# A written order for VectorE, ScalarE and SyncE from the output projection on, and the first down tile multiplied out of the first pool of weights

## The chip, the core and the metric

One core of a Trainium2 chip. The metric is the device time of one execution in microseconds (us). The engines of the core are TensorE (PE, matmuls and transposes), VectorE (DVE), ScalarE (ACT), GpSimd (POOL) and SyncE (SP), which here only issues DMA transfers.

## The reference, cut to what matters

One decoder layer on 256 tokens of width 2048, everything in float32:

```python
h = rmsnorm(x, mix_pre_gain)
q_a, k_a, v_a, q_r, f_r, i_r, g_r = split(h @ w_in)          # 2048 x 5376
attn = rmsnorm(sliding_window_attention(q_a, k_a, v_a, sinks), attn_out_gain)
rnn = hgrn2_chunkwise(q_r, f_r, i_r, g_r, lb, rnn_norm_gain)
mixed = concat([attn, rnn], -1) @ w_out                      # 2048 x 2048
x = x + rmsnorm(mixed, mix_post_gain)
h = rmsnorm(x, mlp_pre_gain)
u = relu(h @ w_up)                                           # 2048 x 8192
y = (u * u) @ w_down                                         # 8192 x 2048
x = x + rmsnorm(y, mlp_post_gain)
```

The change touches the stretch from the last quarter of `@ w_out` to the first products of `@ w_down`.

## The kernel before, in words

**Products in three parts.** Every float32 operand is split into a high part (`whi`, a cast to a shorter format, on ACT, line 90) and a low part (`wlo`, the rest, a subtraction on DVE, line 91). A product is three matmuls: high x high, high x low, low x high (`three`, lines 111 to 113, or `product`, line 785). Weights come in tiles of 512 rows by 512 columns, 1 MB, held as 128 partitions x 4 x 512. Such a raw tile is loaded by a DMA on SP's queue, cast on ACT, subtracted on DVE, and only then can PE use it.

**Tokens.** The 256 tokens are two blocks of 128 (`tb` 0 and 1). `wide_step(o, ch, aT, tb, kt)` multiplies the activations of one block, rows `128*kt` on, by 512 columns of weights into one bank of PSUM: three matmuls. A product of one block over all 2048 rows has 16 such steps, 48 matmuls.

**Output projection (lines 648 to 687).** The 2048 columns are four blocks of 512. The first three are done for both token blocks in turn. From line 660 on PE's order is the written one (`manual_schedule` for PE). The last column block does token block 0, then block 1. `evac_post(c, tb, bank)` squares the bank on ACT for the norm and multiplies it by the gain on DVE into `acc` (tile `mg`, line 608). After the last column `residual(tb)` (line 614) makes the factor (a sum on DVE, a power on POOL, line 600) and adds the scaled rows to `x2` in four DVE steps of 512 columns (line 618), then stores `x2` to memory. `norm2(tb)` (line 635) squares `x2` in four ACT steps (line 589), sums (lines 640, 641), takes a power on POOL (line 642), and makes the normalised rows `hn` in four DVE steps (line 645). `turn(tb, c)` transposes 512 columns of `hn` on PE (four transposes, line 627) into a bank tagged `sc`, casts it to the high part on ACT (line 629) and subtracts for the low part on DVE (line 630), into `h2T`.

**First up chunk (lines 689 to 768).** The 8192 hidden columns are eight chunks of 1024. Of chunk 0, the first 512 columns are multiplied for block 0, then block 1 (`up_w`, loaded at line 689 in half tiles); the next 512 columns (line 745) for both blocks in turn. In between PE turns `hn` of block 0 among the steps 9, 11, 13 and 15 of the last output block, and `hn` of block 1 among the steps 12 to 15 of the first up block. Results pass `relu` (ACT, line 667) and `turn_u` (line 669: four transposes, a square and a cast on ACT, a subtraction on DVE) into `uT`. DVE also makes sums and differences of `hn` (lines 746, 747, 756, 757), since the chunks 1 to 7 use a scheme of seven products for a 2 x 2 block product; `turn_sum` turns these as `s1`, `s2`, `s3`, `s4`.

**Pools of weights.** Up to line 771 weights live in the pool `wpool_a`: 3 raw tiles, 4 `whi`, 4 `wlo`. Then this pool and `phase_b` (with `x2`) are closed, and `wpool_c` opens on the same memory: 2 raw tiles each of the tags `d`, `X`, `P`, `Q`, 3 `whi`, 3 `wlo`. A new tile waits until the old tiles on its memory are done with.

**PSUM.** Eight banks: 3 tagged `pj`, 3 tagged `sc`, 1 `tr`, 1 `o`. A down product of both token blocks holds two banks `sc` from its first tile to its second (`down_half`, line 826).

**Segments (lines 843 to 1036).** From chunk 1 on the work is a list of segments, each one weight tile: up products (`X`, `P`, `Q`, `R`) of 12 matmuls and down tiles (`d`) of 24. From line 1013 on DVE, ACT and SP also follow the written order. For segment k the loop emits: the evictions of k-1 and the additions of raw tiles on DVE, the split of segment k+2 (`prepare`, cast on ACT, subtraction on DVE), evictions on ACT and the turns, the matmuls of k, then loads. Between lines 687 and 1013 the order of DVE, ACT and SP is chosen by a planner with a timing model of its own.

For chunk 1 the list `q` begins with the first down tile `dn[0][0]`, to which the two turns of `s4` are attached, then `m1_first[0]`, `m1_first[1]`, `dn[0][1]`.

Of the kernel before, what the change touches and what calls it, by code (L numbers as in the profile page):

```python
# [29 lines left out]
def tile_hybrid_layer(  # L30
# [36 lines left out]
    def nm(s):  # L67
        uid[0] += 1
        return f"{s}{uid[0]}"
# [110 lines left out]
    def small(shape, tag, bufs=2):  # L180
        return cpool.tile([P] + list(shape), F32, tag=tag, name=nm(tag), bufs=bufs)
# [405 lines left out]
    def square(src, dst):  # L587
        junk = upool.tile([P, 512], F32, tag="u2", name=nm("junk"), bufs=2)
        nc.scalar.activation(out=junk, in_=src, func=AF.Square, scale=D ** -0.5, accum_out=dst)
# [7 lines left out]
    def rsq_part(last, p):  # L597
        r = small([1], "rf")
        nc.vector.tensor_tensor(out=r, in0=last, in1=p, op=ALU.add)
        nc.gpsimd.tensor_tensor(out=r, in0=r, in1=mhalf[:, 0:1], op=ALU.pow)  # L600
        return r
# [11 lines left out]

    def residual(tb):
        r = rsq_part(pss[tb][:, 3:4], ppart[:, tb:tb + 1])
        for c in range(4):
            cs = slice(c * 512, (c + 1) * 512)
            nc.vector.scalar_tensor_tensor(out=x2[tb][:, cs], in0=acc[tb][:, cs], scalar=r, in1=x2[tb][:, cs],
                                           op0=ALU.mult, op1=ALU.add)
        nc.sync.dma_start(out=x2_dram[tb], in_=x2[tb])  # L620
        hn[tb] = keep.tile([P, D], F32, tag=f"acc{tb}", name=nm("hn"))


# [7 lines left out]

    def turn(tb, c):
        turn_act(hn[tb][:, c * 512:(c + 1) * 512], *(h2T[c][:, :, i, tb * P:(tb + 1) * P] for i in range(2)))

    def norm2(tb):
        s2 = small([4], f"s2{tb}")
        for c in range(4):
            square(x2[tb][:, c * 512:(c + 1) * 512], s2[:, c:c + 1])
        st = small([1], "st")
        nc.vector.reduce_sum(out=st, in_=s2, axis=AX.X)  # L640
        nc.vector.tensor_scalar(out=st, in0=st, scalar1=EPS, scalar2=None, op0=ALU.add)
        nc.gpsimd.tensor_tensor(out=rh[:, tb:tb + 1], in0=st, in1=mhalf[:, 0:1], op=ALU.pow)
        for c in range(4):
            cs = slice(c * 512, (c + 1) * 512)
            nc.vector.scalar_tensor_tensor(out=hn[tb][:, cs], in0=x2[tb][:, cs], scalar=rh[:, tb:tb + 1], in1=gpre[c],
                                           op0=ALU.mult, op1=ALU.mult)

    for c in range(3):
        ch = load_wide(w_out_v, 0, c * 512)
# [29 lines left out]
    def new_uT(first="mu0", second="mu1"):  # L679
        return [hpool.tile([P, 4, 2, S], F32R, tag=t, name=nm("uT")) for t in (first, second)]  # L680

    ch = load_wide(w_out_v, 0, 3 * 512, pieces=2)
    banks = [bank("pj"), bank("pj")]
    for kt in range(NKT):
        wide_step(banks[0], ch, mixT, 0, kt)
    evac_post(3, 0, banks[0])
    residual(0)
    norm2(0)
    up_w = load_wide(w_up_v, 0, 0, pieces=2)
    for kt in range(NKT):  # L690
        if kt in (9, 11, 13, 15):
            turn(0, (kt - 9) // 2)
        wide_step(banks[1], ch, mixT, 1, kt)
    evac_post(3, 1, banks[1])
    residual(1)
    norm2(1)


    uT = new_uT()
    ps = [bank("pj"), bank("pj")]  # L700
    for kt in range(NKT):
        if kt in (12, 13, 14, 15):
            turn(1, kt - 12)
        wide_step(ps[0], up_w, h2T, 0, kt)
    u = [new_u(), new_u()]
    relu(u[0], ps[0])
    for kt in range(NKT):
        if kt == 4:
            turn_u(uT, 0, 0, u[0], "tr", 1)
        wide_step(ps[1], up_w, h2T, 1, kt)  # L710
    relu(u[1], ps[1])

# [27 lines left out]
    in_h2T("a22", 1, 1)  # L742
    in_h2T("s4", 1, 0)

    up_w = load_wide(w_up_v, 0, 512)
    nc.vector.tensor_sub(out=tmp, in0=half(1, 0), in1=half(1, 1))
    nc.vector.tensor_sub(out=half(1, 0), in0=half(0, 0), in1=half(1, 0))
    ps = [bank("pj"), bank("pj")]
    for i in range(4):
        for tb in range(2):  # L750
            if i == 0 and tb == 1:
                turn_u(uT, 0, 1, u[1], "tr", 1)
            if i == 1:
                turn_sum(("s1", tmp), tb)
                if tb == 1:
                    nc.vector.tensor_sub(out=tmp, in0=tmp, in1=half(0, 0))
                    nc.vector.tensor_add(out=half(0, 0), in0=half(0, 1), in1=tmp)
            if i == 2:
                turn_sum(("s3", half(1, 0)), tb)
            if i == 3:  # L760
                turn_sum(("s2", tmp), tb)
            for j in range(4):
                wide_step(ps[tb], up_w, h2T, tb, 4 * i + j)
    prev = {}
    for tb in range(2):
        u = new_u()
        relu(u, ps[tb])
        prev[1, tb] = u

    pb.__exit__(None, None, None)  # L770
    pool_w.__exit__(None, None, None)
    wp[0] = ctx.enter_context(tc.tile_pool(name="wpool_c", bufs=2, side="right", reuse_waits="tile"))

    def raw_tile(tag, wv, kt0, c0):
        t = wp[0].tile([P, 4, 512], F32, tag=tag, name=nm(tag), bufs=2)
# [50 lines left out]
    def down_half(ch, c, h, uT, w, tbs=(0, 1), evac=True):  # L826
        if c == 3 and not held:
            held.extend([bank("o", 1), bank("tr", 1)])
        if h == 0 and 0 in tbs:
            down_banks[c] = held if c == 3 else [bank("sc"), bank("sc")]  # L830
        banks = down_banks[c]
        for tb in tbs:
            for j in range(4):
                kt = 4 * h + j
                first = kt == 0 and (c < 3 or ch == 0)
                last = kt == 7 and (c < 3 or ch == NCH - 1)
                three(banks[tb], tok(uT, kt, tb), (w[0][:, j, :], w[1][:, j, :]), first, last)
            if h == 1 and evac:
                evac_down(ch, c, tb, banks[tb])

# [57 lines left out]
    def period(ch, m1_next):  # L900
# [6 lines left out]
        m2 = [up_seg("R", ch, h, "c", lambda: sums["a12"], True) for h in range(2)]  # L907
        dn = [[down_seg(d, c, h) for h in range(2)] for c in range(4)]
        if ch == 1:
            q = [dn[0][0], m1_first[0], m1_first[1], dn[0][1], m5[0], m5[1], dn[1][0], m6[0], m6[1], dn[1][1],  # L910
                 m7[0], m7[1], dn[2][0], m3[0], m3[1], dn[2][1], m4[0], m4[1], m2[0], m2[1],
                 m1_next[0], dn[3][0], m1_next[1], dn[3][1]]
        else:
            q = [m5[0], m5[1], dn[0][0], m6[0], m6[1], dn[0][1], m7[0], m7[1], dn[1][0], m3[0], m3[1], dn[1][1],
                 m4[0], m4[1], dn[2][0], m2[0], m2[1], dn[2][1], m1_next[0], dn[3][0], m1_next[1], dn[3][1]]
# [25 lines left out]
        for k, to, frm, c, h in plan:  # L941
            q[k].adds.append(plus(to, frm, c, h))
        if ch == 1:
            q[0].turns += [lambda c=c: turn_sum(("s4", half(0, 0)), c) for c in range(2)]
            q[1].turns.append(t(d, 1, 0, d))
            q[2].turns.append(t(d, 1, 1, d))
            loads = [(0, "d", d, 1, 0), (1, "d", d, 1, 1), (4, "d", d, 2, 0), (7, "d", d, 2, 1),
                     (8, "R", ch, 0), (9, "R", ch, 1), (10, "d", d, 3, 0), (11, "Q", nx, 0), (12, "Q", nx, 1),
                     (13, "d", d, 3, 1), (14, "X", nx, 0), (15, "X", nx, 1), (16, "P", nx, 0), (17, "P", nx, 1),
                     (19, "d", ch, 0, 0), (21, "d", ch, 0, 1)]  # L950
        else:
            q[0].turns += [t(d, 0, 0, d), t(d, 0, 1, d)]
            q[3].turns.append(t(d, 1, 0, d))
            q[4].turns.append(t(d, 1, 1, d))
            loads = [(0, "d", d, 1, 0), (3, "d", d, 1, 1), (5, "R", ch, 0), (6, "R", ch, 1), (6, "d", d, 2, 0),
                     (9, "d", d, 2, 1), (12, "d", d, 3, 0), (15, "d", d, 3, 1),
                     (17, "d", ch, 0, 0), (19, "d", ch, 0, 1)]
            if nx < NCH:
                loads += [(8, "Q", nx, 0), (9, "Q", nx, 1), (11, "X", nx, 0), (12, "X", nx, 1), (14, "P", nx, 0),
                          (15, "P", nx, 1)]  # L960
# [49 lines left out]
    n_end = len(segs) + len(end)  # L1010
    segs += end + [Seg(lambda h=h: raws["d", last, 3, h], None) for h in range(2)]

    order_all = tc.manual_schedule(engines={mybir.EngineType.DVE, mybir.EngineType.Activation, mybir.EngineType.SP})
    order_all.__enter__()
    load_down(0, 0, 0)
    for h in range(2):
        load_up("X", 1, h)
    load_down(0, 0, 1)
    for h in range(2):
        load_up("P", 1, h)  # L1020

    def prepare(k, between=None):
        segs[k].w = split_weight(None, segs[k].raw(), bufs=3, between=between)

    prepare(0, lambda: [load_up("Q", 1, h) for h in range(2)])
    prepare(1)
    for k in range(n_end):
        x = segs[k]
        for f in (segs[k - 1].dve if k else []) + x.adds:
            f()  # L1030
        prepare(k + 2)
        for f in (segs[k - 1].act if k else []) + x.turns:
            f()
        x.pe(x.w)
        for f in x.loads:
            f()
# [36 lines left out]
```

## Time and profile before

| what | value |
|---|---|
| time, median of 3 runs | 1118.68 us (1118.08 to 1118.79) |
| the profiled execution | 1118.42 us |
| its span, first to last instruction | 1116.7 us |
| mean granted clock of TensorE | 0.990 |
| output projection, last column block, block 0 done | about 396.5 us from the start of the span |
| second token block of the first up block done | about 443 us |
| chunk 0 of the up product done | about 468 us |

How to read the profile: the page's busy times say how long each engine worked, and the chain which work ended last. The table of waits has, for an engine and an operation, what ended its idle time: total, times and longest, in us. A timeline has one line for an instruction, or for several alike in a row: start, duration (of all, first start to last end), engine, line, operation, output <- inputs, shape, count; behind it in brackets the idle time before it and what ended it. Matmuls overlap: the next starts before the last has ended.

### The profile page before, as it was taken

The page shows a single profiled execution, that of the slowest core. Times are in us where ns is not written, and L with a number is a line of the kernel's source. Part 1 is how long each engine was busy: PE and PEld are TensorE (multiplying, and loading weights), DVE is VectorE, ACT ScalarE, POOL GpSimd, SP SyncE. Part 2 cuts the span into 40 slices and gives each one's busy share as a digit, 9 for nine tenths or more (in the row PEclk, how much of TensorE's full clock was granted, in tenths as well). Part 3 has the DMA queues.
Part 4 walks back from the last instruction along what each step waited for, and adds up shares of the span by engine and source line. Part 5 has one row for each costly group of instructions (what it writes and reads, how often), then busy time and mean ns, then how long its engine had stood idle before and what let it go on. Part 6 is the DMA issues. An engine that isn't in the chain of part 4 may idle for free.

```text
span 1116.7 us, 14041 instructions
## 1 busy us (share of the span) xinstructions
PE 1086.6 (97%) x5708; PEld 926.3 (83%) x5708; DVE 846.1 (76%) x765; ACT 623.1 (56%) x719; POOL 19.8 (2%) x48
## 2 busy tenths in 40 slices
PE   8999989999999989899999999999999999999996
PEld 7999889999988867778788888888888888888885
DVE  6755666665655557498998898898898898898565
ACT  6554565545454445455675575575575575575542
POOL 2100000000000000000000000000000000000000
PEclk9999989999999989999999999999999999999999
DMA  8743424444458645726728638638638638534662
GB/s 270 246 164 115 151 76 152 151 151 151 152 190 311 215 158 183 263 83 222 259 92 284 227 99 281 223 103 279 220 108 277 218 112 277 214 114 151 236 253 76
DMA packets 125538, 209.61 MB, mean 188 GB/s; under 512 B 3945, under 2 KB 49570, under 8 KB 124450
## 3 DMA queue, kind: packets, MB, share of 16 engines
q1 hardware_dynamic: 125474, 208.72, 54.7%
q8 instruction: 45, 0.74, 0.3%
q14 instruction: 19, 0.16, 0.0%
HBM read 204.51 MB, written 4.19 MB: 187 GB/s over the span
## 4 chain that ended last, share of the span: by engine, by line
PE 89%; DVE 4%; ACT 2%; issue 1%; DMA 1%; POOL 0%; DVEq 0%; POOLq 0%; ACTq 0%
PE pj L785 21%; PE pj L112 10%; PE pj L113 10%; PE pj L111 10%; PE sc L112 8%; PE sc L111 8%; PE sc L113 8%; DVE wlo L91 2%; PE o L112 1%; PE o L113 1%; PE tr L112 1%; PE tr L113 1%; PE tr L111 1%; PE o L111 1%; ACT whi L90 1%
## 5 line engine op out<-in xcount | busy, mean ns | idle before, releaser
L91 DVE TENSOR_TENSOR wlo<-raw,whi 128x2048 fp32r<-128x2048 f32 (+2 forms) x84 | 152.8, 1832 | 74.6 <-ACT whi L90 74.3
L90 ACT CAST whi<-d 128x2048 fp32r<-128x2048 f32 x60 | 114.8, 1913 | 120.5 <-PE sc L113 85.9
L91 DVE TENSOR_TENSOR wlo<-d,whi 128x2048 fp32r<-128x2048 f32 x60 | 137.4, 2290 | 55.3 <-ACT whi L90 55.2
L90 ACT CAST whi<-raw 128x2048 fp32r<-128x2048 f32 (+2 forms) x84 | 127.8, 1539 | 77.4 <-PE pj L113 38.3
L112 PE MATMUL sc<-wlo,uT 128*128 128x512 f32 x384 | 150.5, 392 | 2.5 <-DVE wlo L91 2.5
L111 PE MATMUL sc<-whi,uT 128*128 128x512 f32 x384 | 150.5, 392 | 2.2 <-ACT whi L90 1.6
L113 PE MATMUL sc<-whi,uT 128*128 128x512 f32 x384 | 150.3, 391 | 0.4 <-DVE uT L677 0.4
L90 ACT CAST whi<-X 128x2048 fp32r<-128x2048 f32 x56 | 107.1, 1915 | 77.9 <-DVE X L789 32.3
L785 PE MATMUL pj<-whi,hT 128*128 128x512 f32 x448 | 143.9, 390 | 0.0
L91 DVE TENSOR_TENSOR wlo<-X,whi 128x2048 fp32r<-128x2048 f32 x56 | 127.9, 2286 | 2.5 <-ACT whi L90 2.5
L111 PE MATMUL pj<-hT,whi 128*128 128x256 f32 x384 | 110.5, 288 | 1.1 <-ACT whi L90 0.7
L113 PE MATMUL pj<-hT,wlo 128*128 128x256 f32 x384 | 110.5, 288 | 0.9 <-DVE wlo L91 0.8
L112 PE MATMUL pj<-hT,whi 128*128 128x256 f32 x384 | 111.2, 290 | 0.0
L785 PE MATMUL pj<-whi,a 128*128 128x512 f32 x336 | 109.9, 395 | 0.0
L785 PEld LDWEIGHTS pj<-whi,hT 128*128 128x128 f32 x448 | 84.1, 188 | 17.4
L112 PEld LDWEIGHTS sc<-wlo,uT 128*128 128x128 f32 x384 | 72.5, 189 | 18.3 <-DVE wlo L91 3.4
L111 PEld LDWEIGHTS sc<-whi,uT 128*128 128x128 f32 x384 | 72.4, 189 | 18.0 <-ACT whi L90 1.8
L785 PE MATMUL pj<-wlo,hT 128*128 128x512 f32 x224 | 87.2, 390 | 0.0
L113 PEld LDWEIGHTS sc<-whi,uT 128*128 128x128 f32 x384 | 72.5, 189 | 15.8 <-DVE uT L677 0.8
L91 DVE TENSOR_TENSOR wlo<-P,whi 128x2048 fp32r<-128x2048 f32 x32 | 73.2, 2291 | 13.8 <-ACT whi L90 13.8
L111 PE MATMUL pj<-whi,hT 128*128 128x512 f32 x192 | 76.0, 398 | 0.0
L111 PEld LDWEIGHTS pj<-hT,whi 128*128 128x128 f32 x384 | 74.1, 193 | 2.0 <-ACT whi L90 0.9
(262 smaller groups left out, 2041.6 us busy)
## 6 DMA issues: line engine op xcount, KB each, us to landing
d<-in_w_down_dram SPq DMA_DIRECT2D x60, 1024.0 KB, 5.0
P<-in_w_up_dram SPq DMA_DIRECT2D x28, 1024.0 KB, 5.5
raw<-in_w_in_dram SPq DMA_DIRECT2D x24, 1024.0 KB, 5.1
raw<-in_w_in_dram SPq DMA_DIRECT2D x35, 512.0 KB, 4.6
raw<-in_w_out_dram SPq DMA_DIRECT2D x16, 1024.0 KB, 5.0
X<-in_w_up_dram SPq DMA_DIRECT2D x14, 1024.0 KB, 5.5
Q<-in_w_up_dram SPq DMA_DIRECT2D x14, 1024.0 KB, 5.4
raw<-in_w_up_dram SPq DMA_DIRECT2D x8, 1024.0 KB, 5.5
```

The source lines that it names most:

```text
L90: nc.scalar.copy(out=hi[:, k], in_=raw[:, k])
L91: nc.vector.tensor_tensor(out=lo[:, k], in0=raw[:, k], in1=hi[:, k].bitcast(F32), op=ALU.subtract)
L111: nc.tensor.matmul(o, lhsT=ah, rhs=bh, start=first, stop=False)
L112: nc.tensor.matmul(o, lhsT=ah, rhs=bl, start=False, stop=False)
L113: nc.tensor.matmul(o, lhsT=al, rhs=bh, start=False, stop=last)
L785: nc.tensor.matmul(o, lhsT=a, rhs=b, start=fresh and kt == 0 and i == 0, stop=kt == 7 and i == 2, skip_group_check=not fresh)
```

## The change

- The written order of DVE, ACT and SP (`order_all`) begins right after the matmuls of the last output column block for token block 0, in place of line 1013.
- `norm2` is dissolved. Its squares, sum and power go into `residual`, each square behind its addition. Its four scalings are now `scaled(tb, c)`, each placed by hand.
- The first up weights are loaded tile by tile (`load_t`), cast and subtracted in halves (`cast_t`, `lo_t`), each half at a written place; every subtraction of a second half issues the load three tiles on. The turns of `hn` move: block 0 behind steps 11, 14 and 16 of the last output block and step 12 of the first up block; block 1 behind step 15 of the first up block and into the steps of its second token block.
- The second 512 columns are split by `split_t`, behind the two subtractions of `hn`; the raw tile of the first down tile is loaded into the first pool, and split there (`w00`) in the third quarter.
- The first down tile is multiplied right after the second 512 columns, before the pool changes. The two relus of chunk 0's second half come behind the first two casts of the new pool (the first relu between them).
- The list of segments begins at `m1_first[0]`. The two turns of `s4` hang on it. A tile "unused" is taken from the tag `whi` of the new pool ahead of the first split. The loads at the start of the new pool are X, X, d, d, P, P in place of d, X, X, d, P, P.

No product is added or left out. The core of the diff:

```diff
@@ -613,11 +613,17 @@
 
     def residual(tb):
         r = rsq_part(pss[tb][:, 3:4], ppart[:, tb:tb + 1])
+        s2 = small([4], f"s2{tb}")
         for c in range(4):
             cs = slice(c * 512, (c + 1) * 512)
             nc.vector.scalar_tensor_tensor(out=x2[tb][:, cs], in0=acc[tb][:, cs], scalar=r, in1=x2[tb][:, cs],
                                            op0=ALU.mult, op1=ALU.add)
+            square(x2[tb][:, cs], s2[:, c:c + 1])
         nc.sync.dma_start(out=x2_dram[tb], in_=x2[tb])
+        st = small([1], "st")
+        nc.vector.reduce_sum(out=st, in_=s2, axis=AX.X)
+        nc.vector.tensor_scalar(out=st, in0=st, scalar1=EPS, scalar2=None, op0=ALU.add)
+        nc.gpsimd.tensor_tensor(out=rh[:, tb:tb + 1], in0=st, in1=mhalf[:, 0:1], op=ALU.pow)
         hn[tb] = keep.tile([P, D], F32, tag=f"acc{tb}", name=nm("hn"))
 
 
...
-    def norm2(tb):
...
@@ -679,36 +672,106 @@
     def new_uT(first="mu0", second="mu1"):
         return [hpool.tile([P, 4, 2, S], F32R, tag=t, name=nm("uT")) for t in (first, second)]
 
+    up_raw, up_w = {}, {}
+
+    def load_t(i):
+        if i < 8:
+            up_raw[i] = load_raw(w_up_v[:, 4 * (i % 4):4 * (i % 4) + 4, (i // 4) * 512:(i // 4 + 1) * 512])
+
+    def cast_t(i, h):
+        if h == 0:
+            up_w[i] = [wp[0].tile([P, 4, 512], F32R, tag=t, name=nm(t), bufs=4) for t in ("whi", "wlo")]
+        k = slice(2 * h, 2 * h + 2)
+        nc.scalar.copy(out=up_w[i][0][:, k], in_=up_raw[i][:, k])
+
+    def lo_t(i, h):
+        k = slice(2 * h, 2 * h + 2)
+        hi, lo = up_w[i]
+        nc.vector.tensor_tensor(out=lo[:, k], in0=up_raw[i][:, k], in1=hi[:, k].bitcast(F32), op=ALU.subtract)
+        if h == 1:
+            load_t(i + 3)
+
+    def split_t(i):
+        up_w[i] = split_weight(None, up_raw[i])
+        load_t(i + 3)
+
+    def scaled(tb, c):
+        cs = slice(c * 512, (c + 1) * 512)
+        nc.vector.scalar_tensor_tensor(out=hn[tb][:, cs], in0=x2[tb][:, cs], scalar=rh[:, tb:tb + 1], in1=gpre[c],
+                                       op0=ALU.mult, op1=ALU.mult)
+
     ch = load_wide(w_out_v, 0, 3 * 512, pieces=2)
     banks = [bank("pj"), bank("pj")]
     for kt in range(NKT):
         wide_step(banks[0], ch, mixT, 0, kt)
+    for i in range(3):
+        load_t(i)
+
+
+    order_all = tc.manual_schedule(engines={mybir.EngineType.DVE, mybir.EngineType.Activation, mybir.EngineType.SP})
+    order_all.__enter__()
     evac_post(3, 0, banks[0])
     residual(0)
-    norm2(0)
-    up_w = load_wide(w_up_v, 0, 0, pieces=2)
-    for kt in range(NKT):
-        if kt in (9, 11, 13, 15):
-            turn(0, (kt - 9) // 2)
-        wide_step(banks[1], ch, mixT, 1, kt)
+    def w3(a, b):
+        for kt in range(a, b):
+            wide_step(banks[1], ch, mixT, 1, kt)
+
+    w3(0, 11)
+    scaled(0, 0)
+    cast_t(0, 0)
+    cast_t(0, 1)
+    lo_t(0, 0)
+    turn(0, 0)
+    scaled(0, 1)
+    w3(11, 14)
+    cast_t(1, 0)
+    lo_t(0, 1)
+    turn(0, 1)
+    w3(14, 16)
+    scaled(0, 2)
+    cast_t(1, 1)
+    lo_t(1, 0)
+    lo_t(1, 1)
+
+
     evac_post(3, 1, banks[1])
+    turn(0, 2)
+    uT = new_uT()
+    for h in range(2):
+        cast_t(2, h)
+        lo_t(2, h)
     residual(1)
-    norm2(1)
-
-
-    uT = new_uT()
+    scaled(0, 3)
     ps = [bank("pj"), bank("pj")]
-    for kt in range(NKT):
-        if kt in (12, 13, 14, 15):
-            turn(1, kt - 12)
-        wide_step(ps[0], up_w, h2T, 0, kt)
+
+    def first(tb, a, b):
+        for kt in range(a, b):
+            wide_step(ps[tb], up4, h2T, tb, kt)
+
+    up4 = [up_w[i] for i in range(3)]
+    first(0, 0, 12)
+    turn(0, 3)
+    for h in range(2):
+        cast_t(3, h)
+        lo_t(3, h)
+    up4.append(up_w[3])
+    first(0, 12, 15)
+    scaled(1, 0)
+    scaled(1, 1)
+    turn(1, 0)
+    first(0, 15, 16)
+    scaled(1, 2)
+    turn(1, 1)
     u = [new_u(), new_u()]
     relu(u[0], ps[0])
-    for kt in range(NKT):
-        if kt == 4:
-            turn_u(uT, 0, 0, u[0], "tr", 1)
-        wide_step(ps[1], up_w, h2T, 1, kt)
-    relu(u[1], ps[1])
+    first(1, 0, 2)
+    scaled(1, 3)
+    turn(1, 2)
+    first(1, 2, 5)
+    turn(1, 3)
+    first(1, 5, 10)
+    turn_u(uT, 0, 0, u[0], "tr", 1)
+    first(1, 10, 16)
 
 
 
@@ -742,34 +805,33 @@
     in_h2T("a22", 1, 1)
     in_h2T("s4", 1, 0)
 
-    up_w = load_wide(w_up_v, 0, 512)
     nc.vector.tensor_sub(out=tmp, in0=half(1, 0), in1=half(1, 1))
     nc.vector.tensor_sub(out=half(1, 0), in0=half(0, 0), in1=half(1, 0))
+    split_t(4)
+    split_t(5)
+    raw00 = load_raw(w_down_v[:, 0:4, 0:512])
+    relu(u[1], ps[1])
     ps = [bank("pj"), bank("pj")]
     for i in range(4):
         for tb in range(2):
             if i == 0 and tb == 1:
                 turn_u(uT, 0, 1, u[1], "tr", 1)
+                split_t(6)
             if i == 1:
                 turn_sum(("s1", tmp), tb)
                 if tb == 1:
                     nc.vector.tensor_sub(out=tmp, in0=tmp, in1=half(0, 0))
+                    split_t(7)
                     nc.vector.tensor_add(out=half(0, 0), in0=half(0, 1), in1=tmp)
             if i == 2:
                 turn_sum(("s3", half(1, 0)), tb)
             if i == 3:
                 turn_sum(("s2", tmp), tb)
+            if i == 2 and tb == 1:
+                w00 = split_weight(None, raw00)
             for j in range(4):
-                wide_step(ps[tb], up_w, h2T, tb, 4 * i + j)
+                wide_step(ps[tb], [up_w[4 + k] for k in range(i + 1)], h2T, tb, 4 * i + j)
     prev = {}
-    for tb in range(2):
-        u = new_u()
-        relu(u, ps[tb])
-        prev[1, tb] = u
-
-    pb.__exit__(None, None, None)
-    pool_w.__exit__(None, None, None)
-    wp[0] = ctx.enter_context(tc.tile_pool(name="wpool_c", bufs=2, side="right", reuse_waits="tile"))
 
     def raw_tile(tag, wv, kt0, c0):
         t = wp[0].tile([P, 4, 512], F32, tag=tag, name=nm(tag), bufs=2)
@@ -838,6 +900,15 @@
             if h == 1 and evac:
                 evac_down(ch, c, tb, banks[tb])
 
+    def relu_first(tb):
+        prev[1, tb] = new_u()
+        relu(prev[1, tb], ps[tb])
+
+    down_half(0, 0, 0, uT, w00, evac=False)
+    pb.__exit__(None, None, None)
+    pool_w.__exit__(None, None, None)
+    wp[0] = ctx.enter_context(tc.tile_pool(name="wpool_c", bufs=2, side="right", reuse_waits="tile"))
+
 
 
     class Seg:
@@ -907,7 +978,7 @@
         m2 = [up_seg("R", ch, h, "c", lambda: sums["a12"], True) for h in range(2)]
         dn = [[down_seg(d, c, h) for h in range(2)] for c in range(4)]
         if ch == 1:
-            q = [dn[0][0], m1_first[0], m1_first[1], dn[0][1], m5[0], m5[1], dn[1][0], m6[0], m6[1], dn[1][1],
+            q = [None, m1_first[0], m1_first[1], dn[0][1], m5[0], m5[1], dn[1][0], m6[0], m6[1], dn[1][1],
                  m7[0], m7[1], dn[2][0], m3[0], m3[1], dn[2][1], m4[0], m4[1], m2[0], m2[1],
                  m1_next[0], dn[3][0], m1_next[1], dn[3][1]]
         else:
@@ -941,10 +1012,10 @@
         for k, to, frm, c, h in plan:
             q[k].adds.append(plus(to, frm, c, h))
         if ch == 1:
-            q[0].turns += [lambda c=c: turn_sum(("s4", half(0, 0)), c) for c in range(2)]
+            q[1].turns += [lambda c=c: turn_sum(("s4", half(0, 0)), c) for c in range(2)]
             q[1].turns.append(t(d, 1, 0, d))
             q[2].turns.append(t(d, 1, 1, d))
-            loads = [(0, "d", d, 1, 0), (1, "d", d, 1, 1), (4, "d", d, 2, 0), (7, "d", d, 2, 1),
+            loads = [(1, "d", d, 1, 1), (4, "d", d, 2, 0), (7, "d", d, 2, 1),
                      (8, "R", ch, 0), (9, "R", ch, 1), (10, "d", d, 3, 0), (11, "Q", nx, 0), (12, "Q", nx, 1),
                      (13, "d", d, 3, 1), (14, "X", nx, 0), (15, "X", nx, 1), (16, "P", nx, 0), (17, "P", nx, 1),
                      (19, "d", ch, 0, 0), (21, "d", ch, 0, 1)]
@@ -1010,20 +1081,21 @@
     n_end = len(segs) + len(end)
     segs += end + [Seg(lambda h=h: raws["d", last, 3, h], None) for h in range(2)]
 
-    order_all = tc.manual_schedule(engines={mybir.EngineType.DVE, mybir.EngineType.Activation, mybir.EngineType.SP})
-    order_all.__enter__()
-    load_down(0, 0, 0)
-    for h in range(2):
-        load_up("X", 1, h)
+    load_up("X", 1, 0)
+    load_up("X", 1, 1)
     load_down(0, 0, 1)
+    load_down(0, 1, 0)
     for h in range(2):
         load_up("P", 1, h)
 
     def prepare(k, between=None):
         segs[k].w = split_weight(None, segs[k].raw(), bufs=3, between=between)
 
+    wp[0].tile([P, 4, 512], F32R, tag="whi", name="unused", bufs=3)
     prepare(0, lambda: [load_up("Q", 1, h) for h in range(2)])
+    relu_first(0)
     prepare(1)
+    relu_first(1)
     for k in range(n_end):
         x = segs[k]
         for f in (segs[k - 1].dve if k else []) + x.adds:
```

More of the change, by code (lines that the diff above doesn't have):

```diff
@@ L633, in turn @@
         turn_act(hn[tb][:, c * 512:(c + 1) * 512], *(h2T[c][:, :, i, tb * P:(tb + 1) * P] for i in range(2)))
-    def norm2(tb):
[L636 to L646, printed above, removed]
     for c in range(3):
```

## The prediction

> **What bounds the kernel now.** I read the page's busy times first, then the table of waits of TensorE (PE) around the edit, then the timelines of PE, VectorE (DVE) and ScalarE (ACT) there.
>
> ```profile
> PE 1086.6 (97%) x5708; PEld 926.3 (83%) x5708; DVE 846.1 (76%) x765; ACT 623.1 (56%) x719; POOL 19.8 (2%) x48
> PE 89%; DVE 4%; ACT 2%; issue 1%; DMA 1%; POOL 0%; DVEq 0%; POOLq 0%; ACTq 0%
> ```
>
> PE is busy for 1086.6 of 1116.7 us, and no matmul is added or removed. So only PE's idle time can change, and the time it spends at a lowered clock. Here is who PE waited for between 380 and 580 us (total, times, longest):
>
> ```profile
> PE sc L627 <- DVE hn L645: 7.7, 2, 5.5
> PE sc L112 <- DVE wlo L91: 2.5, 2, 1.8
> PE sc L111 <- ACT whi L90: 1.6, 1, 1.6
> PE o L112 <- DVE wlo L91: 0.7, 1, 0.7
> PE sc L111 <- DVE hT L630: 0.6, 1, 0.6
> PE sc L113 <- DVE uT L677: 0.4, 1, 0.4
> ```
>
> The first row is the two transposes of the normalised rows (`hn`). The fourth lies behind the edit and stays. The others belong to the first down tiles. Together the five are 12.8 us. PE's timeline shows what follows them:
>
> ```profile
> 402.20 0.39 PE L113 MATMUL pj<-whi,mu 128*128 128x512 f32 x1
> 408.13 1.12 PE L627 MATMUL sc<-ident,hn 128*128 128x128 f32 x4 [5.54 <-DVE hn L645]
> ...
> 409.90 0.63 PE L113 MATMUL pj<-whi,mu 128*128 128x512 f32 x1
> 410.32 0.63 PE L111 MATMUL pj<-whi,mu 128*128 128x512 f32 x1
> ...
> 427.24 0.63 PE L627 MATMUL sc<-ident,hn 128*128 128x128 f32 x4 [2.12 <-DVE hn L645]
> ...
> 468.31 1.03 PE L627 MATMUL sc<-ident,hn 128*128 128x128 f32 x8
> 470.95 0.50 PE L111 MATMUL sc<-whi,uT 128*128 128x512 f32 x1 [1.60 <-ACT whi L90]
> 473.27 0.50 PE L112 MATMUL sc<-wlo,uT 128*128 128x512 f32 x1 [1.82 <-DVE wlo L91]
> ...
> 474.66 0.63 PE L113 MATMUL sc<-whi,uT 128*128 128x512 f32 x1
> 475.08 0.63 PE L111 MATMUL sc<-whi,uT 128*128 128x512 f32 x1
> ```
>
> and the chain of work gives the full-clock price of a group:
>
> ```profile
> 414.00 0.44 PE sc L627 x4
> ...
> 505.74 5.44 PE pj L785 x24
> ```
>
> At full clock a matmul takes 5.44/24 = 0.227 us and a turn (four transposes) 0.44. After the wait of 5.54, and after 1.60 and 1.82 close together, matmuls start 0.42 apart: the clock is halved. After 2.12 alone it is not (the matmuls behind it last 0.39, not 0.63). The first halving costs six matmuls 0.2 late each and two turns some 1.0 late, 2.2 us; the second nine matmuls, 1.8. The view also counts a wait from the modelled end of a matmul, 0.39 after its start, though the next could start after 0.227: 0.16 more for each of seven waits, 1.1. Lost today, in the part that is edited: 12.8 + 4.0 + 1.1 = **17.9 us**. That is all the change could win.
>
> **The change, stage 1: from the output projection's last block to the first up block.** Now DVE and ACT run in written order, so I follow each queue. Durations:
>
> ```profile
> 397.89 0.15 DVE L599 TENSOR_TENSOR rf<-pss,ppart 128x1 f32<-128x1 f32 x1
> 398.70 2.74 DVE L618 SCALAR_TENSOR_TENSOR x<-mg,rf,x 128x512 f32<-128x512 f32 x4 [0.66 <-POOL rf L600]
> ...
> 404.04 2.36 DVE L91 TENSOR_TENSOR wlo<-raw,whi 128x1024 fp32r<-128x1024 f32 x2 [0.33 <-ACT whi L90]
> ...
> 421.75 2.74 DVE L618 SCALAR_TENSOR_TENSOR x<-mg,rf,x 128x512 f32<-128x512 f32 x4 [0.65 <-POOL rf L600]
> ...
> 425.54 0.15 DVE L641 TENSOR_SCALAR st<-st 128x1 f32<-128x1 f32 x1
> 426.35 2.74 DVE L645 SCALAR_TENSOR_TENSOR hn<-x,rh,gpre 128x512 f32<-128x512 f32 x4 [0.66 <-POOL rh L642]
> 429.00 0.68 DVE L630 TENSOR_TENSOR hT<-sc,hT 128x512 fp32r<-128x512 f32 x1
> ```
> ```profile
> 402.98 1.97 ACT L90 CAST whi<-raw 128x1024 fp32r<-128x1024 f32 x2
> ...
> 427.91 0.59 ACT L629 CAST hT<-sc 128x512 fp32r<-128x512 f32 x1 [2.60 <-PE sc L627]
> ```
>
> *First turn, the gain.* In token block 0 ACT made weight casts between the squares; block 1 shows the chain without them: first `x` 421.75 to first `hn` 426.35, 4.60 us. The new order puts the squares first, so `hn` starts at 398.70 + 4.60 = 403.3, and the transposes 0.89 later (426.35 to 427.24), at 404.2. PE, done with step 8 at 402.4, now runs two more steps (six matmuls, 1.36) and arrives at 403.8. It waits 0.4 in place of 5.54, and keeps its clock.
>
> *Turns 2 and 3.* Between two turns DVE does: one half split (1.18), the low half of the turned tile (0.68, which starts 0.67 + 0.59 after the transposes: 427.24 to 427.91 and the cast), one scaling (0.69). Turn 2 is ready at 407.0, PE at 404.2 + 0.44 + nine matmuls = 406.7: 0.3. Turn 3 is ready at 409.8, PE at 408.8: 1.0.
>
> *Turn 4.* DVE now has, ahead of `scaled(0,3)`: that scaling, four half splits (4.72), the product of the eviction and a low half (1.37), until 415.7; then the whole of `residual(1)`: 0.81 to the first `x` (397.89 to 398.70) and 3.94 to the end of the sum (421.75 to 425.54 + 0.15). It starts at 420.5, the turn at 421.4. PE has done 36 matmuls by 409.8 + 0.44 + 8.17 = 418.5. It waits 2.9.
>
> *Fourth weight tile.* Its casts are queued on ACT behind turn 4's cast: 0.67 + 0.59 after the transposes, a half cast (0.99), then a half split (1.18). PE is free 0.44 after the transposes start, so it idles 1.8, does one matmul, and idles 0.95 more: 2.8 together. Before, this tile was cast and split well ahead of its use.
>
> *The second token block* then follows with the scalings in time. Sum of waits 0.4 + 0.3 + 1.0 + 2.9 + 2.8 = 7.4; since successive DVE steps start about 0.06 before the listed end of the last (two halves take 2.36, four scalings 2.74 where single ones overlap), 6.5 is the lower end and I take **7.0**, against 7.7 before.
>
> POOL's four small powers keep their places. On SP the weight loads now wait for half splits in the written order, one `x2` store ahead of the seventh:
>
> ```profile
> raw<-in_w_up_dram SPq DMA_DIRECT2D x8, 1024.0 KB, 5.5
> ```
>
> Loads four to six leave at about 408, 412 and 416 and land 5.5 us later; their casts come at 422, 437 and 439, so this costs nothing. If that slack went, each late load would cost its lateness once.
>
> **Stage 2: second up block.** Two subtractions for the sums now precede the split of tile 4 on DVE, behind the low half of the first `turn_u`:
>
> ```profile
> 429.60 1.22 DVE L746 TENSOR_TENSOR tmp<-hn 128x1024 f32<-128x1024 f32 x1
> ...
> 436.66 2.29 DVE L91 TENSOR_TENSOR wlo<-raw,whi 128x2048 fp32r<-128x2048 f32 x1 [2.72 <-ACT whi L90]
> 438.87 0.69 DVE L677 TENSOR_TENSOR uT<-u,uT 128x512 fp32r<-128x512 f32 x1
> ```
> ```profile
> 434.73 1.91 ACT L90 CAST whi<-raw 128x2048 fp32r<-128x2048 f32 x1 [2.15 <-PE pj L113]
> 436.54 0.59 ACT L674 ACTIVATE u<-tr 128x512 f32<-128x512 f32 x1
> 437.16 0.62 ACT L676 CAST uT<-u 128x512 fp32r<-128x512 f32 x1
> ```
>
> From the start of that turn: 0.67, square 0.62, cast 0.62, low half 0.69, two subtractions 2.44, split 2.29: 7.3. PE from the same point: 0.44 and 19 matmuls, 4.75. A new wait of **2.5** (2.3 to 2.7); the fixed order makes it, since before, the subtractions ran at 429.6, under the first block.
>
> **Stage 3: first down tiles.** Let T be the end of the second up block (468.31 before). The first down tile (24 matmuls, 5.44) now runs straight from T, its weights split in stage 2: the waits of 1.60, 1.82, 0.64 and, with one split less in DVE's queue, 0.36 and 0.66 go. But the two turns for `s4` are moved behind it, when its two banks hold two of the three banks tagged `sc`. Both turns and the next `turn_u` must share the third. And DVE reaches the low half of the first only after the splits of X0 and X1, an addition and the split of the next down tile:
>
> ```profile
> 478.74 2.28 DVE L789 TENSOR_TENSOR X<-X,P 128x2048 f32<-128x2048 f32 x1
> ```
>
> With X0 cast just by T, that is 4 x 2.25 + 0.68 = T + 9.7. PE is free at T + 5.44 + 0.44 = T + 5.9 and must wait for that bank: 3.8. If the third cast of the new pool lies on the memory that the first down tile's weights occupied (the tile named "unused" shifts the others off it), it starts after T + 5.6 and the low half ends at T + 5.6 + 1.91 + 2.29 + 0.68 = T + 10.5: 4.6. I take 4.2. The second `s4` turn then holds the bank for 0.67 + 0.59 + 0.68 and some 0.1 of hand-over, less its own 0.44: 1.6 more before `turn_u`. **5.8** (5.4 to 6.2). The additional load P0 has to land before T + 4.5; it may wait for the raw tile of the first down tile, free about T - 4, and lands 5.5 later, at T + 1.5: hidden with 3 us to spare.
>
> **Clock.** The pairs 2.9 + 2.8 and 4.2 + 1.6 are both longer than the 1.60 + 1.82 that halved the clock. From two rows, 1.8 and 2.2, two halvings cost about 4.0 at most; since PE comes back part-way through a slow stretch, down to 1.5; I take 2.4. [...]
>
> **Sum.** After: 7.0 + 2.5 + 5.8 + 2.4 = 17.7 against 17.9. The profiled execution took 1118.42 (span 1116.7 and 1.7 around it), 0.26 below the median of 1118.68. Forecast 1118.42 - 0.2 = **1118.2 us**, no change. By the ends (6.5 + 2.3 + 5.4 + 1.5 = 15.7 and 7.4 + 2.7 + 6.2 + 4.0 = 20.3) 1116.2 to 1120.8. A measurement tells about 0.2%, 2.2 us, from no change.
>
> **The rivals.** *The s4 turns do not hold PE up* (DVE is ahead of T, or a bank is free): 5.8 and one halving, 1.2, go: 1111.2. For it: DVE is the only reason, and it idles at times before T. Against: X0's cast stands on ACT behind the last turn of stage 2, and the table shows PE already waiting for this bank (0.6, `hT` L630). 0.13. *The clock stays up in both places*: 1118.2 - 2.4 = 1115.8. For: 2.12 left it alone. Against: 1.60 + 1.82 did not. 0.08. *All new waits are hidden*: 1118.4 - 17.9 = 1100.5; for it only that every step could have been ordered earlier. 0.04. *Slower: the second cast (X1) is the one that lies on the first down tile's weights.* Then it starts at T + 5.6, and behind it come 1.91, its split 2.29, addition, split (4.5) and 0.68: T + 15.0, 4.9 above the value taken, 1123.1. It decides if "unused" shifts by one slot too few; against it, that tile is there at all. 0.10. *Slower by the clock's upper end* with both ends of the waits: 1120.8. 0.07.
>
> **How the numbers follow.** The forecast keeps 0.58, of which 0.54 within 0.2%, the rest split to both sides. Faster: 0.13 + 0.08 + 0.04 + 0.02 = 0.27; slower: 0.10 + 0.07 + 0.02 = 0.19; same 0.54. The likeliest case alone spans 1116.2 to 1120.8. Leaving out 1100.5 and 1123.1 (0.14), the range is 1111.0 to 1121.0.
>
> **What would show it.** Right: the 5.5 us wait for `hn` shrinks to under 1; new waits of 2 to 3 for the fourth `hn` turn and for ACT's cast behind it; about 2.5 for the split before the second up block; none before the first down tile; 4 and 1.6 before the second `s4` turn and the `turn_u`. Wrong: no wait on `sc` behind the first down tile, or a wait above 8 there.

## The result, and the profile after

The changed kernel takes 1129.01 us (median of 4 runs, 1128.76 to 1129.14) against 1118.74 (4 runs, 1118.08 to 1119.39): ratio 1.0092, 95% interval 1.008 to 1.0105. It is slower by 0.9%. The forecast was 1118.2, the range 1111.0 to 1121.0. The profiled execution took 1129.14 us, its span is 1127.4 us.

Who PE waited for, between 380 and 600 us of the changed kernel (total, times, longest):

```profile
PE sc L633 <- DVE hT L636: 11.2, 1, 11.2
PE sc L633 <- DVE hn L700: 3.2, 3, 2.2
PE pj L112 <- DVE wlo L91: 2.4, 1, 2.4
PE pj L111 <- ACT whi L685: 1.6, 1, 1.6
PE sc L665 <- DVE hT L636: 1.4, 1, 1.4
PE pj L112 <- DVE wlo L690: 0.8, 1, 0.8
PE o L112 <- DVE wlo L91: 0.5, 1, 0.5
```

The 5.5 us wait for `hn` is gone, and so are the waits of the first down tile. The waits of 2.2 (in the second row), 1.6 with 0.8, and 2.4 are the ones that the forecast set. The first row is not: 11.2 where 4.2 was forecast.

*Where the time went, by stage.* Both kernels issue the same number of matmuls before the same point, so the starts of a few of them can be set side by side. First PE's timeline of the changed kernel: the first matmul of the last output block's second token block, of the second up block, of the first down tile, and of the fourteenth segment of the old list (a `Q` product):

```profile
397.21 0.39 PE L111 MATMUL pj<-whi,mu 128*128 128x512 f32 x1
...
442.39 0.39 PE L111 MATMUL pj<-whi,hT 128*128 128x512 f32 x1
...
471.73 0.39 PE L111 MATMUL sc<-whi,uT 128*128 128x512 f32 x1
...
538.21 0.39 PE L847 MATMUL pj<-whi,hT 128*128 128x512 f32 x1
```

and of the kernel before, the first, second and last of these; the third is the start of its `s4` turns, 468.31, shown above:

```profile
396.30 0.39 PE L111 MATMUL pj<-whi,mu 128*128 128x512 f32 x1
...
443.18 0.39 PE L111 MATMUL pj<-whi,hT 128*128 128x512 f32 x1
...
527.42 0.39 PE L785 MATMUL pj<-whi,hT 128*128 128x512 f32 x1
```

The changed kernel is 0.9 us late before the edit begins (397.21 against 396.30). Executions differ by nearly as much: among the profiles of the experiments, which share all code up to there, this matmul starts anywhere from 395.3 to 397.0. From there stage 1 gains 1.7 (45.18 against 46.88), stage 2 loses 4.2 (29.34 against 25.13), stage 3 loses 7.4 (66.48 against 59.11). The first of these is the least sure: in the profiles of E1 to E5 below, with the same code in stage 1, it takes 45.9 to 46.4, and so gains 0.5 to 1.0. Behind stage 3 the distance stays: 10.8 at 538 us, 10.7 at the end of the span.

*What the 11.2 us are.* PE's timeline of the changed kernel behind the first down tile:

```profile
477.18 0.60 PE L633 MATMUL sc<-ident,hn 128*128 128x128 f32 x4
488.94 1.12 PE L633 MATMUL sc<-ident,hn 128*128 128x128 f32 x4 [11.17 <-DVE hT L636]
491.46 1.12 PE L665 MATMUL sc<-ident,u 128*128 128x128 f32 x4 [1.40 <-DVE hT L636]
```

ACT and DVE at the same time:

```profile
469.18 0.59 ACT L635 CAST a<-sc 128x512 fp32r<-128x512 f32 x1 [2.62 <-PE sc L633]
477.38 1.90 ACT L90 CAST whi<-X 128x2048 fp32r<-128x2048 f32 x1 [7.61 <-PE sc L113]
```
```profile
479.31 4.58 DVE L91 TENSOR_TENSOR wlo<-X,whi 128x2048 fp32r<-128x2048 f32 x2 [8.82 <-ACT whi L90]
483.80 2.28 DVE L851 TENSOR_TENSOR X<-X,P 128x2048 f32<-128x2048 f32 x1
486.00 2.29 DVE L91 TENSOR_TENSOR wlo<-d,whi 128x2048 fp32r<-128x2048 f32 x1
488.20 0.68 DVE L636 TENSOR_TENSOR hT<-sc,hT 128x512 fp32r<-128x512 f32 x1
```

Read from the bottom. The second `s4` turn (488.94) waits for the bank that the first one filled, until DVE has made its low half (488.20). DVE has this behind the splits of X0 and X1, the addition and the split of the next down tile, as the forecast said. But the whole queue starts at 479.31, not about T = 471.7, since ACT's very first cast of the new pool, X0, stood idle for 7.6 us until the last matmul of the first down tile (`sc L113`) was done. The forecast had X0 cast by T and let only a later cast wait for that tile.

### The profile page after: what moved, and what is told of

Its sections match the earlier page's. It is cut to its first block, busy times and chain, and to the rows that moved or that the text cites. A ratio compares the mean times of both kernels' runs of the same rounds, so it can differ in the third digit from the quotient of the medians.

```text
span 1127.4 us, 14033 instructions
## 1 busy us (share of the span) xinstructions
PE 1090.8 (97%) x5708; PEld 930.1 (82%) x5708; DVE 846.3 (75%) x765; ACT 622.6 (55%) x719; POOL 20.5 (2%) x48
## 4 chain that ended last, share of the span: by engine, by line
PE 90%; DVE 4%; DMA 3%; ACT 2%; issue 1%; SPq 0%; POOL 0%; DVEq 0%; POOLq 0%; ACTq 0%
PE pj L847 22%; PE pj L112 10%; PE pj L113 10%; PE pj L111 10%; PE sc L111 8%; PE sc L112 8%; PE sc L113 8%; DVE wlo L91 2%; DMA raw<-in_w_in_dram 1%; PE o L112 1%; PE tr L113 1%; PE o L113 1%; PE tr L111 1%; PE tr L112 1%; PE o L111 1%; ACT whi L90 1%
## 5 line engine op out<-in xcount | busy, mean ns | idle before, releaser
L91 DVE TENSOR_TENSOR wlo<-raw,whi 128x2048 fp32r<-128x2048 f32 (+2 forms) x77 | 145.6, 1902 | 71.2 <-ACT whi L90 71.0
L91 DVE TENSOR_TENSOR wlo<-d,whi 128x2048 fp32r<-128x2048 f32 x59 | 135.1, 2289 | 49.2 <-ACT whi L90 49.1
L90 ACT CAST whi<-raw 128x2048 fp32r<-128x2048 f32 (+2 forms) x77 | 121.7, 1596 | 69.3 <-PE pj L113 33.2
L113 PE MATMUL sc<-whi,uT 128*128 128x512 f32 x384 | 149.4, 389 | 0.0
L847 PE MATMUL pj<-whi,hT 128*128 128x512 f32 x448 | 145.3, 393 | 0.0
L113 PE MATMUL pj<-hT,wlo 128*128 128x256 f32 x384 | 110.7, 288 | 0.4 <-DVE wlo L91 0.4
L847 PE MATMUL pj<-wlo,hT 128*128 128x512 f32 x224 | 87.9, 392 | 0.0
L113 PEld LDWEIGHTS sc<-whi,uT 128*128 128x128 f32 x384 | 72.1, 188 | 14.9
L112 PE MATMUL pj<-wlo,hT 128*128 128x512 f32 x192 | 76.9, 403 | 3.1 <-DVE wlo L91 2.4
L111 PE MATMUL pj<-whi,hT 128*128 128x512 f32 x192 | 77.1, 404 | 1.6 <-ACT whi L685 1.6
```

Of the source, the lines that this page charges most:

```text
L90: nc.scalar.copy(out=hi[:, k], in_=raw[:, k])
L91: nc.vector.tensor_tensor(out=lo[:, k], in0=raw[:, k], in1=hi[:, k].bitcast(F32), op=ALU.subtract)
L111: nc.tensor.matmul(o, lhsT=ah, rhs=bh, start=first, stop=False)
L112: nc.tensor.matmul(o, lhsT=ah, rhs=bl, start=False, stop=False)
L113: nc.tensor.matmul(o, lhsT=al, rhs=bh, start=False, stop=last)
L847: nc.tensor.matmul(o, lhsT=a, rhs=b, start=fresh and kt == 0 and i == 0, stop=kt == 7 and i == 2, skip_group_check=not fresh)
```

## The experiments

The theory (A): X0's high part lies in the memory where the high part of the first down tile's weights (`w00`) lay. The tile "unused" is there to prevent this, but nothing reads or writes it, and so it takes no place. The rivals: (B) all of the new pool waits until the old one is closed, behind the first down tile; (C) the bank and DVE's queue are the whole loss, and X0's cast does not matter.

**E1: the tile takes its place.**

```diff
-    wp[0].tile([P, 4, 512], F32R, tag="whi", name="unused", bufs=3)
+    hold = wp[0].tile([P, 4, 512], F32R, tag="whi", name="hold", bufs=3)
+    nc.gpsimd.memset(hold[:, 0, 0:8].bitcast(F32), 0.0)
```

> The changed kernel, but the tile named unused gets one user, a memset of eight columns on GpSimd, so that it really takes a place in the tag whi. Theory A (memory): in the changed kernel X0's cast waited for the first down tile's matmuls because its high tile lay where that tile's high weights lay; a tile without a user takes no place. Then X0's cast now starts about 2 us before the second up block ends, only the third cast waits for the first down tile, and PE's wait before the second s4 turn falls from 11.2 to between 4 and 6; total 1121 to 1124. Theory B (pool): everything in the new pool waits until the old one is closed behind the first down tile; then the wait stays near 11 and the time at 1128 to 1130.

1122.86 us (5 runs), ratio to before 1.0035 [1.0022, 1.0049]. ACT's timeline, X0's cast and the third cast, then PE's:

```profile
469.85 1.91 ACT L90 CAST whi<-X 128x2048 fp32r<-128x2048 f32 x1
...
477.73 1.90 ACT L90 CAST whi<-d 128x2048 fp32r<-128x2048 f32 x1 [3.17 <-POOL hold L1095]
```
```profile
482.61 1.12 PE L633 MATMUL sc<-ident,hn 128*128 128x128 f32 x4 [4.64 <-DVE hT L636]
485.13 1.11 PE L665 MATMUL sc<-ident,u 128*128 128x128 f32 x4 [1.40 <-DVE hT L636]
...
490.99 0.60 PE L665 MATMUL sc<-ident,u 128*128 128x128 f32 x4
```

and POOL's, the memset:

```profile
477.60 0.10 POOL L1095 MEMSET hold<- 128x8 f32 x1 [56.51 <-PE sc L113]
```

X0 is cast right behind the last turn of stage 2, and only the third cast waits (for `hold`, which now has the place on `w00`: its memset is what waits for the last matmul of the first down tile). PE's waits are 4.64 and 1.40; the forecast's upper bound for this arrangement was 4.6 and 1.6. B falls, A stands: the misplaced tile costs 6.2 us (1129.01 - 1122.86). But this is the arrangement that the forecast had in mind, and it still takes 4.7 us more than the forecast, 1118.2, and more than the top of its range, 1121.0. So the tile is not the whole miss.

**E4: the line taken out.**

```diff
-    wp[0].tile([P, 4, 512], F32R, tag="whi", name="unused", bufs=3)
```

> The changed kernel without the line that takes the tile named unused. Theory A (memory, the tile without a user takes no place): nothing changes, X0's cast waits for the first down tile as before and the time is 1128 to 1130. Rival: the line shifts the places, and without it another cast waits; then the 11.2 us wait changes by more than 2.

One run, 1128.34 us. PE's longest wait, and X0's cast:

```profile
PE sc L633 <- DVE hT L636: 11.2, 1, 11.2
```
```profile
476.48 1.90 ACT L90 CAST whi<-X 128x2048 fp32r<-128x2048 f32 x1 [7.63 <-PE sc L113]
```

The same picture to 0.1 us: the line does nothing in the changed kernel.

**E2: the s4 turns first**, the tile "unused" as it was.

```diff
-            q[1].turns += [lambda c=c: turn_sum(("s4", half(0, 0)), c) for c in range(2)]
...
+    for c in range(2):
+        turn_sum(("s4", half(0, 0)), c)
     down_half(0, 0, 0, uT, w00, evac=False)
```

> The changed kernel with the two s4 turns put ahead of the first down tile, in the order of every engine; the tile named unused as it was. Theory A (memory): X0's cast still waits for the first down tile's matmuls, about 5.4 us after the second up block and the turns; PE waits 2 to 4 before turn_u and the first up products instead of 11.2 and 1.4 for the s4 turns; total 1120 to 1124. Theory C (bank): the bank and VectorE's queue ahead of s4's low half are the whole loss; then no wait over 1 is left there and the time is 1114 to 1117.

1122.12 us (8 runs), ratio 1.0025 [1.0015, 1.0036]. X0's cast and PE's waits in this stage:

```profile
478.60 1.90 ACT L90 CAST whi<-X 128x2048 fp32r<-128x2048 f32 x1 [4.85 <-PE sc L113]
```
```profile
PE sc L665 <- ACT u L660: 2.5, 1, 2.5
...
PE sc L113 <- DVE uT L670: 1.1, 1, 1.1
```

The waits for the bank are gone, but X0's cast still waits, and behind it on ACT the relu (L660) for which the next turn waits. So C falls as well: the order of the turns and the place of X0 each cost.

**E3: both edits**, the diffs of E1 and E2 together.

> Both edits: the tile takes its place, and the s4 turns go ahead of the first down tile. Theory A (both count): the waits of 11.2 and 1.4 go, the splits of X0 and X1 lie under the first down tile, and what is left is VectorE being late for the second half of the next down tile, 2 to 3 us; total 1115 to 1118. Theory C (bank alone): the same time as with the turns moved alone. Theory B (pool): the same too.

1117.63 us (10 runs), ratio 0.9984 [0.9975, 0.9994]: level with the kernel before, at the edge of what can be told. PE's waits:

```profile
PE sc L633 <- DVE hn L700: 3.2, 3, 2.2
PE pj L112 <- DVE wlo L91: 2.4, 1, 2.4
PE sc L113 <- DVE uT L670: 2.0, 1, 2.0
PE pj L111 <- ACT whi L685: 1.6, 1, 1.6
PE o L112 <- DVE wlo L91: 0.6, 1, 0.6
PE pj L112 <- DVE wlo L690: 0.6, 1, 0.6
```

In stage 3 only a wait of 2.0 for a low half of `uT` is left, behind DVE's additions and splits. The two mends together give 11.4 us; alone they give 6.2 and 6.9, more in sum, since they shorten the same wait.

**E5: stages 1 and 2 alone.** The first down tile goes back into the new pool and to the head of the list, with its turns, its loads and the two relus; the line "unused" goes. The edits of the loads, the relus and that line are not shown:

```diff
-    raw00 = load_raw(w_down_v[:, 0:4, 0:512])
...
-                w00 = split_weight(None, raw00)
...
-    down_half(0, 0, 0, uT, w00, evac=False)
...
-            q = [None, m1_first[0], m1_first[1], dn[0][1], m5[0], m5[1], dn[1][0], m6[0], m6[1], dn[1][1],
+            q = [dn[0][0], m1_first[0], m1_first[1], dn[0][1], m5[0], m5[1], dn[1][0], m6[0], m6[1], dn[1][1],
...
-            q[1].turns += [lambda c=c: turn_sum(("s4", half(0, 0)), c) for c in range(2)]
+            q[0].turns += [lambda c=c: turn_sum(("s4", half(0, 0)), c) for c in range(2)]
```

> Stages 1 and 2 of the change alone: the written order and the half tiles up to the end of chunk 0's up products; the first down tile is loaded into the new pool, heads the list of segments and carries the s4 turns, as before the change. The forecast's steps: stage 1 gains 1 to 2 us, stage 2 loses the new wait of 2.4 and the half clock seen behind it, some 4; the down tiles' waits of 1.6, 1.8 and 0.6 are back. Theory A (all the rest of the loss is stage 3): total 1120 to 1123. Theory D (the early stages leave a backlog that is paid later): 1125 or more.

1122.00 us (7 runs), ratio 1.0027 [1.0016, 1.0037]. The first two stages cost 3 us net, and nothing of them is paid later: D falls. (In its profile stage 3 takes 59.08 us, against 59.11 in the kernel before.) Stage 3 as changed costs 7.0 more (1129.01 - 1122.00); with both mends it gains 4.4 (1117.63 - 1122.00).

**E6: the split ahead of the first `turn_u` and of the subtractions**, on top of E3.

```diff
     first(1, 5, 10)
+    split_t(4)
     turn_u(uT, 0, 0, u[0], "tr", 1)
...
-    split_t(4)
     split_t(5)
```

> The kernel with both mends (the tile takes its place, the s4 turns first), and in addition the split of the fifth up tile moved ahead of the first turn_u, and so ahead of the two subtractions. If the subtractions are what makes the second up block wait: the wait of 2.4 goes, and the half clock behind it, 2.4 to 4 us together, total 1113 to 1115.5. Rival: VectorE's work is only moved and the wait comes back at the next tiles; total 1116 to 1118.

1113.72 us (5 runs), ratio 0.9953 [0.994, 0.9965]. PE's waits:

```profile
PE sc L633 <- DVE hn L700: 3.2, 3, 2.2
PE sc L113 <- DVE uT L670: 1.9, 1, 1.9
PE pj L111 <- ACT whi L685: 1.6, 1, 1.6
PE pj L112 <- DVE wlo L690: 0.8, 1, 0.8
PE sc L112 <- DVE wlo L91: 0.7, 1, 0.7
PE o L112 <- DVE wlo L91: 0.6, 1, 0.6
```

The row of 2.4 is gone; one row of 0.7 is new, and one has grown by 0.2. Stage 2's loss was the place of this split, 3.9 us with the slow matmuls behind the wait. The edit moves the split ahead of the first `turn_u` as well as of the subtractions, so it does not tell the two apart. In the changed kernel ACT starts the split's cast at 439.67, behind the casts of that turn, and such a cast lasts 1.91; DVE starts the split at 442.80. So without the subtractions it could have started about 1.2 us sooner, half of the wait; this is an estimate, not a run.

**E7: the last scaling of token block 0 ahead of the residual**, on top of E6.

```diff
-    residual(1)
     scaled(0, 3)
+    residual(1)
```

> The kernel before this one, and the last scaling of token block 0 put ahead of the residual of token block 1 on VectorE. The wait of 2.2 before the fourth turn goes; the casts of the fourth weight tile stand behind that turn's cast, which now stands behind the residual's squares on ScalarE, so the wait for them grows by about 1: net gain 1 to 1.5 us, total 1111.5 to 1114.5. Rival: the residual is later by as much and the second token block waits for it: no gain.

1111.92 us (5 runs), ratio 0.9939 [0.9925, 0.9952]: the fastest version, faster than both kernels. PE's waits:

```profile
PE pj L111 <- ACT whi L685: 2.7, 1, 2.7
PE sc L113 <- DVE uT L670: 2.0, 1, 2.0
PE sc L633 <- DVE hn L700: 0.9, 2, 0.8
PE pj L112 <- DVE wlo L690: 0.8, 1, 0.8
PE sc L112 <- DVE wlo L91: 0.7, 1, 0.7
PE o L112 <- DVE wlo L91: 0.7, 1, 0.7
```

The 2.2 before the fourth turn goes, 1.1 of it comes back in the wait for the fourth tile's cast (1.6 to 2.7): a gain of 1.8, a little over the 1 to 1.5 that was expected. The listed waits sum to 1.0 less than in E6; the other 0.8 is not assigned to a cause. No new wait of the second token block is listed, so the rival falls.

## Why the prediction was wrong, point by point

**What bounds the kernel** held: PE's busy time is nearly the same (1090.8 us after, 1086.6 before), and all differences are waits and clock (mean granted clock 0.982 after, 0.990 before).

**Stage 1** held in its waits. First turn: 0.4 forecast, 0.17 measured. Second: 0.3 against no row. Third: 1.0 against 0.76. Fourth: 2.9 against 2.22. Fourth tile: 2.8 against 1.62 + 0.76. The listed ends of DVE's steps may have made each term a little long; this was not tested. The forecast net gain was 2.0 (10.2 lost before, with the 0.16 of two waits, against 7.0 and one halved clock at 1.2); measured 1.7 in this profile and 0.5 to 1.0 in those of E1 to E5; the slow stretch cost 1.4 here and 2.4 in E1, in place of 1.2 (worked out below).

**Stage 2** held in its wait, 2.5 against 2.4, and E6 shows that it hangs on the place of the split. The size was off: the stage lost 4.2, since the clock was halved behind this single wait (granted clock 0.50 from 445.1 to 448.4 us), for which the forecast had put nothing.

**Stage 3** is where it failed first, at the step "With X0 cast just by T". The forecast named the memory of the first down tile's weights, but put a later cast on it, because "the tile named "unused" shifts the others off it". It does not (E4), and the first cast of the queue waits. Everything that the forecast placed behind it (two splits, an addition, a split, the low half) was right in order and length, only 7.6 us later on ACT: 11.2 in place of 4.2. The second wait, 1.6 forecast, was 1.4.

**The rivals.** The slower rival had the mechanism with the wrong cast, X1 in place of X0, 4.9 us above the value taken in place of 7.0, and 1123.1 in place of 1129.0. Its argument against itself, "that tile is there at all", was no row of the profile but a reading of what a line is for. The three faster rivals did not come about: the bank did hold PE up, the clock did fall, and stages 1 and 2 kept new waits. Of the last rival the clock's part came and was passed: about 6 us against its 4.0.

**Clock.** This is the second step that failed: two halvings were forecast for 2.4 us, with 4.0 at most; three came (in the changed kernel at a granted clock of 0.50, from 424.6 to 428.0, from 445.1 to 448.4 and from 482.7 to 496.2 us), and cost about 6. The 2.4 was an estimate between 1.5 and 4.0, taken from the kernel before (granted clock 0.50 from 405.6 to 412.4 us, with PE back at 408.13, and from 473.9 to 477.2); no run shows that value: the slow stretches cost about 6 here and 7.2 in E1. The price of a slow stretch is the time from start to start, less 0.227 for each matmul and 0.44 for each turn in it. In the changed kernel the stretch behind the fourth weight tile's waits cost 1.4 (seven matmuls from 425.11 to 428.15), the one behind stage 2's wait 1.7, and the one behind the 11.2 us some 2.8: one turn and twelve matmuls from 491.46 to 496.95, 2.3 too long, and the second `s4` turn before them, about 0.5 (its transposes took 1.12 in place of 0.60). In E1 the three cost 2.4, 1.6 and 3.2, 7.2 together; the last is 2.7 between the rows of 485.13 and 490.99 shown there, and again 0.5 for the turn.

**Sum.** Forecast -0.2. Measured by stage -1.7 + 4.2 + 7.4, and 0.9 from ahead of the edit: 10.8. By medians the miss is 10.8 too (1129.01 - 1118.2). The misplaced cast is 6.2 of it (E1). The other 4.7 is left in E1, and worked out from its rows it is nearly all the clock: E1's eight new waits sum to 13.7, or about 15 with 0.16 for each as in the forecast's count, against 7.0 + 2.5 + 5.8 = 15.3 forecast; the clock cost 7.2 against 2.4.

## What to carry to other kernels

A tile that is requested and never used need not take a place (with the line for "unused" 1129.01 us, without it 1128.34): ask of each new tile whose memory it lies on and when that is released, above all for the first instruction of a fixed queue, since all behind it pay (here the 7.6 us by which ACT's first cast was late). When a turn is moved behind work that holds the banks, look up what stands on the evicting engine's queue before its eviction. Count a chance of a halved clock behind each single wait like the one of 2.4 us here, and not only behind pairs of waits (five profiles of six, 1.5 to 1.7 us). A written order takes the planner's freedom away, so an operation that fills a gap (here two subtractions, with a turn's eviction) has to be placed behind what PE needs next.

## What the runs showed of the hardware that was not expected

Behind a single wait of 2.4 us the clock was halved in some profiles and not in another. Six profiles have this wait, and five of them show slow matmuls behind it (the changed kernel, E1, E2, E3 and E5). In the changed kernel the matmuls behind it are listed with 0.63 and start 0.43 apart for 3 us, where 0.39 and 0.227 are the figures at full clock; the granted clock is 0.50 from 445.1 to 448.4 us:

```profile
445.14 0.80 PE L112 MATMUL pj<-wlo,hT 128*128 128x512 f32 x1 [2.37 <-DVE wlo L91]
...
446.16 0.63 PE L111 MATMUL pj<-whi,hT 128*128 128x512 f32 x1
446.59 0.63 PE L112 MATMUL pj<-wlo,hT 128*128 128x512 f32 x1
...
448.62 0.39 PE L111 MATMUL pj<-whi,hT 128*128 128x512 f32 x1
```

In E1, E2, E3 and E5 PE is back at full clock first, and the slow starts come 0.8 to 1.5 us later. In E4, with the same code there and a wait as long, they do not come, and the granted clock is 1.00 from 435 to 449 us:

```profile
445.78 0.50 PE L112 MATMUL pj<-wlo,hT 128*128 128x512 f32 x1 [2.38 <-DVE wlo L91]
446.12 0.40 PE L113 MATMUL pj<-whi,hT 128*128 128x512 f32 x1
```

The price can be read off the starts: from 445.14 to 448.62 there are eight matmuls, which take 1.8 us at full clock and took 3.5, so 1.7 us. In E4 stage 2 takes 27.83 us, against 29.34 to 29.42 in the other five, which puts the price at 1.5 to 1.6. So the outcome depends on more than the length of the wait: with the same code, 2.37 us was followed by a slow stretch and 2.38 was not. On what else it depends was not shown. For this kernel a new wait of 2.4 us should be costed with a chance of 1.5 to 1.7 us on top (five profiles of six here); the single wait of 2.12 in the kernel before cost none (granted clock 1.00 from 424 to 430 us).
